# Query and key projections by Strassen's scheme in a stage of their own, behind the values

## The chip, the cores and the metric

The kernel runs on one core of a Trainium2 chip. The engines are TensorE (PE: matmuls, with PEld for its weight loads), VectorE (DVE), ScalarE (ACT), GpSimd (POOL) and SyncE (SP, which here only issues DMAs). The time is that of one execution on the device, in microseconds; lower is better.

## The reference

One layer of a decoder trunk, 1024 tokens by 1024 channels, float32. Only the first half of the layer matters here. One projection of the normalised input gives everything that the mixer needs:

```python
h = rms_norm(x, pre_mix_g[l])
proj = h @ w_in[l]                         # (1024, 1024) @ (1024, 8192)
qa, ka, va, qb, kb, vb, gates = jnp.split(proj, split_at, axis=-1)
qa = apply_rope(qa.reshape(b, s, A_HEADS, 2, A_QK_DIM), cos_a, sin_a)     # 4 heads, 2 x 64
ka = apply_rope(ka.reshape(b, s, A_HEADS, 2, A_QK_DIM), cos_a, sin_a)
...
oa = diff_attention(qa, ka, va, lam)       # causal (softmax1 - lam * softmax2) @ v
...
qb = apply_rope(qb.reshape(b, s, B_GROUPS, B_HEADS, B_HEAD_DIM), cos_b, sin_b)   # 3 groups, 4 heads of 128
kb = apply_rope(kb.reshape(b, s, B_GROUPS, B_HEADS, B_HEAD_DIM), cos_b, sin_b)
...                                        # windows (128, 512, 2048) with dilation (1, 4, 16)
mix = (g_a * ya + g_b * yb) @ w_mix_out[l] # g_a, g_b: sigmoid of the gates
x = x + rms_norm(mix, post_mix_g[l])
...                                        # then a gated MLP with a short convolution
```

So queries and keys are 2 x 512 columns for attention A and 2 x 1536 for attention B: 32 blocks of 128 columns. The gates are 16 more blocks.

## The kernel before

Every float32 product is made of three matmuls with operands split in two parts: high (a rounded copy, made by ScalarE) and low (the rest, a subtraction by VectorE). `split` makes both parts, `mm3` (lines 153 to 157) issues the three matmuls high x high, low x high and high x low.

The program is written in order, and a scheduler turns it into one fixed stream of instructions for each engine, by a simulated time line and by priorities (`high_priority`), and by explicit ties (`issue_after`: an instruction may be placed only after another one). At run time each engine works through its stream in order and waits on semaphores. A tile pool hands out a fixed number of buffers for each tag; a write into a buffer waits until the last reader of its earlier content is done.

The stages up to the mixer's output are these.

- The values (lines 445 to 654). The 2048 value columns are computed by Strassen's scheme: seven products of half-sized blocks in place of eight. The input x stands transposed in SBUF, split in `xh` and `xl`, channels in two halves and tokens in two halves: blocks b11, b12, b21, b22. The scheme needs sums of these blocks. They are t2, t3, t4 in tiles of their own, and t1, which takes the place of b12. At the end of this stage b12 is loaded and split again (`again`), because all that follows needs the plain x. The norms of the rows, the rotation tables (`tab_d`) and the softmax weight lambda are made beside it. The values go to HBM (`v_d`).
- Queries, keys and gates (`proj_t`, lines 232 to 244). A block of 128 columns is computed in two halves of 512 tokens, each a sum over eight channel blocks: 2 x 8 x 3 = 48 matmuls of 128x512, with weights in `load_unit`, loaded by SP and split. A yield after every six matmuls lets a caller interleave it with other work.
- Attention A (`attend_a`, from line 749): four heads, each with eight blocks of 128 query rows in the order 6, 7, 4, 5, 2, 3, 0, 1. A job is one such block: scores into two PSUM buffers, mask and minimum (VectorE), two exponentials (ScalarE), the weighted difference (VectorE). Its transposes, splits and products with the values follow one to two jobs later (`later`).
- Attention B (`attend_b`, from line 950): twelve steps (two pairs of heads, three groups, two heads), each with four jobs of two row blocks, and a merge of the three groups' results by their log-sums.
- The output projections, the mixer and the MLP. The MLP's up projection uses Strassen's scheme too (`seven`, from line 1437), with 84 matmuls to a step.

The order around the change is this. While attention A works on head h, `interleave` puts the projections of head h+1 (`proj_a`) and three gates between the jobs, in proportion to weights; in attention B it puts the projections of the next step (`proj_b`). Queries and keys go from PSUM through `rotated` (a copy of swapped halves by ScalarE; two products with the tables and a sum by VectorE) and are split straight into the SBUF tiles that the scores read. These tiles, the values of a pair of heads and the raw values come from one pool of 18 buffers (`slot`). Gates are stored to HBM (`gt_d`) and read again by the output projections. The distribution of the gates is written by hand:

```python
START_GATES, A_FILLS, B_GATES = 1, ("gpgg", "gpvgg", "wgpgg", "xgPVgg"), 3
```

Here p and P stand for projections, g for a gate, v and x for loads of values, w and V for splits of them.

## Time and profile before

| | |
|---|---|
| median of 3 runs | 1696.86 us (1695.76 to 1697.7) |
| the profiled execution | 1697.3 us, span 1695.3 us |
| TensorE busy | 1682.1 us, 99% of the span, 8078 matmuls |
| VectorE busy | 1333.5 us, 79%, 2445 instructions |
| ScalarE busy | 891.8 us, 53%, 1663 instructions |
| GpSimd busy | 106.3 us, 6%, 174 instructions |
| HBM traffic | 167.05 MB read, 47.86 MB written |
| TensorE's mean granted clock | 0.998 |

A line of the profile names the engine and the line of the kernel, the tile written and the tiles read ("acc<-xh,whi": the accumulator from x's high part and a weight's high part), the shape, and how often it ran. A line can be that of a helper: L155 to L157 are the three matmuls of `mm3`, wherever it was called; L149 and L146 are the copy and the subtraction of `split`. "<-" behind an idle time names what ended it. Busy time is the union of an engine's instructions; matmuls of 128x512 overlap, so a sum of their durations is more than the time that they take. In a table of stretches the columns are the stretch, its length, the busy time and number of instructions of each engine, the granted clock, the share of the DMA engines' time and GB/s.

### The profile page before, as it was taken

The page shows a single profiled execution, that of the slowest core. Times are in us where ns is not written, and L with a number is a line of the kernel's source. Part 1 is how long each engine was busy: PE and PEld are TensorE (multiplying, and loading weights), DVE is VectorE, ACT ScalarE, POOL GpSimd, SP SyncE. Part 2 cuts the span into 40 slices and gives each one's busy share as a digit, 9 for nine tenths or more (in the row PEclk, how much of TensorE's full clock was granted, in tenths as well). Part 3 has the DMA queues.
Part 4 walks back from the last instruction along what each step waited for, and adds up shares of the span by engine and source line. Part 5 has one row for each costly group of instructions (what it writes and reads, how often), then busy time and mean ns, then how long its engine had stood idle before and what let it go on. Part 6 is the DMA issues. An engine that isn't in the chain of part 4 may idle for free.

```text
span 1695.3 us, 22960 instructions
## 1 busy us (share of the span) xinstructions
PE 1682.1 (99%) x8078; PEld 1410.0 (83%) x8078; DVE 1333.5 (79%) x2445; ACT 891.8 (53%) x1663; POOL 106.3 (6%) x174
## 2 busy tenths in 40 slices
PE   9999999999999999999999999999999999999997
PEld 7888888888888888888888888888888888888886
DVE  8795686877776766677756865899999989799967
ACT  7643575656454776666653533464444445355453
POOL 0031000000000000000123400300000000000000
PEclk9999999999999999999999999999999999999999
DMA  8677311214112213233585631132222222296524
GB/s 266 234 253 235 99 60 62 86 59 119 50 63 81 70 53 108 86 112 119 200 285 186 203 118 63 38 106 92 95 81 75 98 83 88 95 343 214 193 75 161
DMA packets 104451, 216.41 MB, mean 128 GB/s; under 512 B 12992, under 2 KB 22144, under 8 KB 104336
## 3 DMA queue, kind: packets, MB, share of 16 engines
q1 hardware_dynamic: 89296, 171.28, 30.5%
q0 software_dynamic: 10288, 35.28, 6.1%
q10 hardware_dynamic: 4752, 8.39, 1.3%
q8 instruction: 63, 1.03, 0.3%
q14 instruction: 52, 0.43, 0.1%
HBM read 167.05 MB, written 47.86 MB: 127 GB/s over the span
## 4 chain that ended last, share of the span: by engine, by line
PE 97%; DMA 2%; DVE 1%; ACT 1%; issue 0%; SPq 0%; DVEq 0%
PE acc L155 22%; PE acc L156 22%; PE acc L157 22%; PE acc L1578 3%; PE acc L1579 3%; PE acc L1577 3%; PE o L710 2%; PE pt L697 2%; PE acc L1258 2%; PE acc L1256 2%; PE acc L1257 2%; PE o L713 1%; PE s L156 1%; PE s L157 1%; PE s L155 1%; PE s L768 1%
## 5 line engine op out<-in xcount | busy, mean ns | idle before, releaser
L156 PE MATMUL acc<-xh,wlo 128*128 128x512 f32 x768 | 303.2, 395 | 0.0
L157 PE MATMUL acc<-xl,whi 128*128 128x512 f32 x768 | 303.1, 395 | 0.0
L155 PE MATMUL acc<-xh,whi 128*128 128x512 f32 x768 | 303.0, 395 | 0.0
L149 ACT ACTIVATE whi<-raw 128x512 fp32r<-128x512 f32 (+1 forms) x252 | 156.1, 626 | 170.3 <-PE acc L157 88.1
L146 DVE TENSOR_TENSOR wlo<-raw,whi 128x512 fp32r<-128x512 f32 (+1 forms) x252 | 178.8, 717 | 40.4 <-ACT whi L149 34.7
L156 PEld LDWEIGHTS acc<-xh,wlo 128*128 128x128 f32 x768 | 144.4, 188 | 27.8
L157 PEld LDWEIGHTS acc<-xl,whi 128*128 128x128 f32 x768 | 144.5, 188 | 27.5
L155 PEld LDWEIGHTS acc<-xh,whi 128*128 128x128 f32 x768 | 144.4, 188 | 27.3
L155 PE MATMUL acc<-mh,whi 128*128 128x512 f32 x400 | 155.8, 390 | 0.3 <-ACT mh L149 0.3
L156 PE MATMUL acc<-mh,wlo 128*128 128x512 f32 x400 | 155.6, 389 | 0.0
L157 PE MATMUL acc<-ml,whi 128*128 128x512 f32 x400 | 155.3, 389 | 0.0
L684 ACT ACTIVATE t<-acc 64x512 f32<-64x512 f32 (+1 forms) x160 | 94.7, 592 | 55.3 <-PE acc L157 53.3
L1454 DVE TENSOR_TENSOR u<-acc,u 128x512 f32<-128x512 f32 x133 | 91.3, 691 | 20.3 <-PE acc L157 20.1
L149 ACT ACTIVATE whi<-s 128x512 fp32r<-128x512 f32 x76 | 46.9, 627 | 102.3 <-PE acc L157 88.1
L685 DVE TENSOR_TENSOR t<-acc,cos 128x512 f32<-128x512 f32 x64 | 44.1, 690 | 67.1 <-ACT t L684 63.5
L155 PEld LDWEIGHTS acc<-mh,whi 128*128 128x128 f32 x400 | 75.1, 188 | 16.0 <-ACT mh L149 0.5
L156 PEld LDWEIGHTS acc<-mh,wlo 128*128 128x128 f32 x400 | 75.1, 188 | 15.6
L157 PEld LDWEIGHTS acc<-ml,whi 128*128 128x128 f32 x400 | 75.1, 188 | 15.5
L1578 PE MATMUL acc<-whi,wlo 128*128 128x512 f32 x220 | 77.6, 390 | 0.0
L1577 PE MATMUL acc<-whi 128*128 128x512 f32 x220 | 76.4, 389 | 0.0
L1579 PE MATMUL acc<-wlo,whi 128*128 128x512 f32 x220 | 73.2, 390 | 0.0
L777 ACT ACTIVATE s<-s,mx 128x896 f32<-128x896 f32 (+7 forms) x64 | 49.4, 772 | 36.9 <-DVE mx L770 21.0
(387 smaller groups left out, 3941.6 us busy)
## 6 DMA issues: line engine op xcount, KB each, us to landing
raw<-in_w_in SPq DMA_DIRECT2D x96, 256.0 KB, 2.9
raw<-in_w_up SPq DMA_DIRECT2D x88, 256.0 KB, 2.8
raw<-in_w_v SPq DMA_DIRECT2D x71, 256.0 KB, 4.7
raw<-c_d SPq DMA_DIRECT2D x48, 256.0 KB, 3.8
c_d<-c SPq DMA_DIRECT2D x22, 512.0 KB, 2.7
raw<-in_w_down SPq DMA_DIRECT2D x37, 256.0 KB, 4.1
v_d<-yv POOLq DMA_DIRECT2D x32, 256.0 KB, 4.5
gt_d<-gate ACTq DMA_DIRECT2D x32, 256.0 KB, 2.1
```

Of the source, the lines that this page charges most:

```text
L146: eng.tensor_tensor(lo, src, hi.bitcast(F32), op=ALU.subtract)
L149: copy = nc.scalar.activation(hi, src, AF.Copy)
L155: nc.tensor.matmul(o, sh, mh, start=first, stop=False, skip_group_check=on)
L156: nc.tensor.matmul(o, sl, mh, start=False, stop=False, skip_group_check=on)
L157: nc.tensor.matmul(o, sh, ml, start=False, stop=last, skip_group_check=on)
L684: nc.scalar.activation(t1[dst], ps[src], AF.Copy)
L685: nc.vector.tensor_tensor(t2, ps, cos[:, sl], op=ALU.mult)
L777: exp = nc.scalar.activation(sc[c][:, :w], sc[c][:, :w], AF.Exp, bias=mx[:, c, 0:1], scale=-1.0, accum_out=den[:, c : c + 1])
L1454: nc.vector.tensor_tensor(to, made(p), x, op=ALU.add)
L1577: nc.tensor.matmul(banks[m], gh[:, tk], wh, start=f == 0, stop=False)
L1578: nc.tensor.matmul(banks[m], gl[:, tk], wh, start=False, stop=False)
L1579: nc.tensor.matmul(banks[m], gh[:, tk], wl, start=False, stop=f == NH - 1)
```

## The change

The projections of queries and keys leave the attention stages and become one stage between the values and attention A.

- The stage works on 16 pairs, a query block and its key block: four heads of A, then twelve of B in the order of their use. A pair's 256 columns by 1024 tokens are computed by Strassen's scheme (`seven_q`): seven products of 4 x 3 matmuls with the blocks of x that the values used, t1 still in the place of b12. Two products add to a bank of another (p2 on p1, p3 on p5). So the loading and splitting of b12 moves from the end of the values to the end of this stage.
- The sums of weight blocks are made by DMA. SP loads a11, a12, a22 and a21; ScalarE writes negated copies; DMAs that accumulate, issued by GpSimd, add blocks: s1 = a21 + a22, s3 = a11 - a21, s2 = s1 - a11, s4 = a12 - s2 (`sums_a` two pairs ahead, `sums_b` one). Pair 0's are begun in the last steps of the values, and its weights split there. Seven weight tiles of a pair are split while the pair before is computed (`put_w`).
- A pair's results are rotated in SBUF (`rotate_q`, tiles of 128x1024) and split and stored to HBM (`store_q`, into the new `qk_d`) while the next pair is computed. For this the rows of w_in's query and key blocks are permuted on the host for heads of A, and unpermuted by the store.
- `in_turn` ties the stage's ScalarE and VectorE instructions to each other in the written order; only the evictions stand outside of it, with a higher priority.
- The attention stages load queries and keys from `qk_d` (`load_a`: twelve DMAs of 64 rows; `load_b`: four of 512 KB), one head or step ahead.
- The gates are the only projections left between the jobs. They are handed out in pieces of six matmuls: 8 before attention A, 16 in each of its heads, 4 or 5 in each step of B. A piece is tied behind the first score matmuls of the job before the last (`scored`, `issue_after`).
- The products with the values alternate between two pools of PSUM (`outs`). The rotation tables lie in a pool that is open from the start.

```diff
-START_GATES, A_FILLS, B_GATES = 1, ("gpgg", "gpvgg", "wgpgg", "xgPVgg"), 3
+START_GATES, B_GATES = 8, (4, 5, 4, 5, 5, 5, 4, 5, 5, 5, 4, 5)
+A_FILLS = ("gpggg", "gpgvgg", "wgpggg", "xgPgVgg")
...
+    qk_d = dram.tile([2 * (AH + BG * BH), 2, P, S], F32, name="qk_d")
...
+    outs = itertools.cycle([lambda: psum(F32, ps_o, "o"), psum])
...
+    def in_turn():
+        with ExitStack() as stack:
+            for ins in tail.values():
+                stack.enter_context(tc.issue_after(ins))
+            last = nc.cur_bb.bb.instructions[-1]
+            yield
...
+                if ins.engine in (nc.scalar.engine, nc.vector.engine):
+                    tail[str(ins.engine)] = ins
...
+        def sums_a(n):
+            d11, d12, d21, d22 = quarters(n)
+            to = sums_q[n] = {"a11": load_raw(d11, "raw"), "s1": begin(d21), "a22": load_raw(d22, "t1"), "a12": load_raw(d12, "t2")}
+            to["s3"] = begin(to["s1"], -1.0)
+            to["s2"] = begin(to["a11"], -1.0)
+            add_to(to["s1"], d22)
+            add_to(to["s3"], d11)
+            add_to(to["s2"], to["s1"])
...
+        def put_w(n, *names):
+            for name in names if n < len(pairs) else ():
+                t = ws_q.setdefault(n, {})[name] = next(slots_q)()
+                split(*t, sums_q[n][name])
...
-            if (p, i) == ("p5", 1):
-                again.append(load_raw(a["xT"][k][:, 512:], next(tags)))
-            if (p, i) == ("p6", 1):
-                with behind_marks():
-                    split_x(k, halves()[1], again[k])
...
+        ops_q = dict(p1=("a11", b11), p6=("s2", t2), p2=("a12", b21), p7=("s3", t3), p5=("s1", b12), p4=("a22", t4), p3=("s4", b22))
...
+        def rotate_q(n, c, u):
+            sw = pq.tile([P, S], F32, tag="sw", name="sw", bufs=2)
+            for src, dst in ((up_half, low_half), (low_half, up_half)):
+                nc.scalar.activation(sw[dst], u[src], AF.Copy)
+            nc.vector.tensor_tensor(u, u, tab[0], op=ALU.mult)
+            nc.vector.tensor_tensor(sw, sw, tab[1], op=ALU.mult)
+            nc.vector.tensor_tensor(u, u, sw, op=ALU.add)
...
+            m1 = made("p1")
+            copy(c11, m1)
+            yield
+            m4 = made("p4")
+            made("p2", m1)
+            m6 = made("p6")
+            add(c12, m6, c11)
+            copy(c11, m1)
+            yield
+            m7 = made("p7")
+            add(c22, m7, c12)
+            add(c21, m4, c22)
+            yield
+            m5 = made("p5")
+            add(c22, m5, c22)
+            yield us
+            made("p3", m5)
+            add(c12, m5, c12)
+            yield
...
+            next(made_q)
+            if n:
+                next(before)
+                with in_turn():
+                    rotate_q(n - 1, 1, old[1])
+            with in_turn():
...
+                put_w(n + 1, "a11")
+                for m, fn in ((n + 1, sums_b), (n + 2, sums_a)) if n else ((2, sums_a),):
+                    if m < len(pairs):
+                        fn(m)
+            if n:
+                with in_turn():
+                    store_q(n - 1, 1, old[1])
...
+            if n == len(pairs) - 1:
+                again = [load_raw(a["xT"][k][:, 512:], t) for k, t in enumerate(("raw", "t1", "t2", "raw"))]
+                with in_turn():
+                    for k in range(4):
+                        split_x(k, halves()[1], again[k])
...
+    def load_a(h, res):
...
+            dma(f32(to), src)
...
+                with tc.issue_after(scores[0]) if scores[0] else nullcontext():
+                    piece = next(supply, None)
...
+    def load_b(g, h, res):
+        ops = [slot(n) for n in ("qh", "ql", "kh", "kl")]
...
+            dma(f32(t), qk_d[at + n // 2, n % 2])
...
-        fill = proj_b(nxt[1], nxt[2], ops_b[nxt], functools.partial(split_b, *nxt[:2]) if h % 2 else None)
-        interleave(jobs(todo), 4, (itertools.chain(fill, once(load_ots)) if nxt == steps[-1] else fill, 8))
+        fills = [(once(functools.partial(load_b, *nxt[1:], ops_b[nxt])), 0), gates(B_GATES[n] // 2)]
+        if h % 2:
+            fills.append((once(functools.partial(split_b, *nxt[:2])), 0))
+        fills.append(gates(B_GATES[n] - B_GATES[n] // 2))
```

248 lines of the change are left out of this document (168 added, 80 removed).

## The prediction

> **What bounds the kernel now.** I read the page's engine totals and its chain first, then the table of stretches over the stages that the change touches, then the rows of single tiles in those stretches.
>
> ```profile
> PE 1682.1 (99%) x8078; PEld 1410.0 (83%) x8078; DVE 1333.5 (79%) x2445; ACT 891.8 (53%) x1663; POOL 106.3 (6%) x174
> ...
> PE 97%; DMA 2%; DVE 1%; ACT 1%; issue 0%; SPq 0%; DVEq 0%
> ```
>
> TensorE is busy for 99% of the span and is 97% of the chain that ended last. So a matmul that goes away is worth its time, as long as nothing else becomes late. The stretches are the values (to 162 us), the first gate and head 0's projections (to 204), differential attention (to 504) and dilated attention (to 864); columns are length, busy time by engine, clock, DMA share, GB/s.
>
> ```profile
> 0.00:162.00 162.00, 158.92 (x689) 130.46 (x690) 130.63 (x229) 89.87 (x154) 23.77 (x46) 1.00 0.74 245
> 162.00:204.00 42.00, 42.00 (x187) 34.80 (x186) 20.00 (x31) 22.15 (x37) 2.47 (x6) 1.00 0.42 133
> 204.00:504.00 300.00, 300.00 (x1570) 256.15 (x1569) 228.62 (x585) 174.20 (x364) 0.00 (x0) 1.00 0.23 73
> 504.00:864.00 360.00, 360.00 (x1985) 309.49 (x1984) 248.59 (x566) 233.33 (x500) 22.20 (x38) 1.00 0.34 112
> ```
>
> From 162 to 864 us, 702 us, TensorE has no idle time at all at full clock. VectorE (DVE) has 76% and 69% of the two attention stretches.
>
> The same table restricted to the accumulators "acc" counts the projection's matmuls in the attention stretches (PE is the second number):
>
> ```profile
> 204.00:504.00 300.00, 235.88 (x944) 172.62 (x943) 27.53 (x40) 33.07 (x56) 1.00 0.23 73
> 504.00:864.00 360.00, 293.74 (x1174) 213.35 (x1173) 33.71 (x49) 52.20 (x88) 1.00 0.34 112
> ```
>
> Busy times of pipelined matmuls overlap, so the price is the distance of their starts:
>
> ```profile
> 265.69 0.39 PE L156 MATMUL acc<-xh,wlo 128*128 128x512 f32 x1
> ...
> 269.33 0.39 PE L157 MATMUL acc<-xl,whi 128*128 128x512 f32 x1
> ```
>
> These are the first and last of 17 in a row: 3.64 us over 16 steps, 0.2275 us each. Differential attention then holds 944 x 0.2275 = 214.8 us of projections and 85.2 us of its own; dilated attention 267.1 and 92.9 us. This is the filler: 6.7 us for each of 32 jobs (4 heads x 8 row blocks), 5.6 us for each of 48 (12 steps x 4).
>
> **The change part by part.** *Matmuls removed.* Queries and keys are 32 column blocks of 2 x 8 x 3 = 48 matmuls, 1536. A pair (query and key block) becomes seven products of 4 x 3 matmuls, 84 in place of 96, so 16 x 84 = 1344. 192 go, all of 128x512: 192 x 0.2275 = 43.7 us. The gates stay 16 x 48. New TensorE time for this part: 305.8 (new stage) + 174.7 (gates) + 178.1 (attention) = 658.6, against 702. A gain beyond 43.7 us is excluded, since TensorE had no idle time in these stretches to win back.
>
> *The new stage: who keeps up.* A pair has 84 x 0.2275 = 19.1 us of TensorE. DVE's prices come from back-to-back starts:
>
> ```profile
> 1314.46 0.69 DVE L1454 TENSOR_TENSOR u<-acc,u 128x512 f32<-128x512 f32 x1
> 1315.06 0.68 DVE L146 TENSOR_TENSOR wlo<-raw,whi 128x512 fp32r<-128x512 f32 x1
> ```
> ```profile
> 609.01 2.36 DVE L146 TENSOR_TENSOR vl<-vperm,vh 128x1024 fp32r<-128x1024 f32 x2
> 611.29 0.55 DVE L146 TENSOR_TENSOR pt<-pt 128x384 fp32r<-128x384 f32 x1
> ```
> ```profile
> 602.05 1.21 DVE L878 TENSOR_TENSOR ql<-t,qh 128x512 fp32r<-128x512 f32 x1
> 603.15 0.70 DVE L146 TENSOR_TENSOR wlo<-raw,whi 128x512 fp32r<-128x512 f32 x1
> ```
>
> So 0.60 us for 512 columns, 1.14 for 1024, 1.10 for 512 read with a stride. A pair has 7 weight splits and 5 evicting adds (12 x 0.60 = 7.2), 6 rotation operations and 2 store splits of 1024 columns (8 x 1.14 = 9.1): 16.3 us, 85% of 19.1. For the eight pairs with dilation 4 or 8 the store splits are strided, 2.2 us each: 7.2 + 6.8 + 4.4 = 18.4 us, 96%. Is that enough? The kernel has such a stage, the same 84 matmuls to a step, in its up projection:
>
> ```profile
> 1110.00:1180.00 70.00, 70.00 (x310) 57.76 (x309) 69.97 (x100) 34.98 (x54) 0.81 (x9) 1.00 0.30 106
> 1180.00:1250.00 70.00, 70.00 (x311) 57.98 (x309) 66.07 (x90) 30.06 (x40) 0.80 (x8) 1.00 0.26 87
> ```
>
> There TensorE loses nothing beside a DVE that is 100% and 94% busy. If DVE lost its overlap (durations 0.69, 1.18, 2.3 in place of starts), a strided pair would need 8.3 + 7.1 + 4.6 = 20.0 us, 0.9 too much, 7 us over eight pairs. I take 3, nearer to the up projection's row; ends 0 and 7. ScalarE:
>
> ```profile
> L149 ACT ACTIVATE whi<-raw 128x512 fp32r<-128x512 f32 x40 | 25.1, 629 | 15.2 <-PE acc L157 14.7
> ...
> L149 ACT ACTIVATE vh<-vperm 128x1024 fp32r<-128x1024 f32 x6 | 6.3, 1051 | 0.1
> ```
>
> 12 operations of 512 columns (7 splits, 2 evictions, 3 negated sums) and 6 of 1024 (4 half-swaps, 2 store copies): 7.5 + 6.3 = 13.8 us, some 2 us more with strides, 72 to 83%. It hides. The sums ride on DMAs. Accumulating ones aren't in this trace; the nearest rows:
>
> ```profile
> raw<-in_w_in SPq DMA_DIRECT2D x96, 256.0 KB, 2.9
> ...
> v_d<-yv POOLq DMA_DIRECT2D x32, 256.0 KB, 4.5
> ...
> ot<-oa_d SPq DMA_DIRECT2D x4, 512.0 KB, 4.0
> ```
>
> s1 is a load and one accumulate, s2 one more: 2.9 + 4.5 + 4.5 = 11.9 us (2.9 + 2 x 2.9 = 8.7 at the lower end), and ScalarE needs s2, to begin s4, one iteration (19.1 us) after the issue. So I cost them at nothing, hidden by one pair of TensorE. POOL issues four per pair; in the values they stand behind the stores to v_d, with one whole pair before s2 is due. Stage traffic is 4 MB in 19.1 us, 210 GB/s, against 245 in the values: it fits.
>
> *Start and end of the stage.* Pair 0's first sums and seven splits (7 x 0.60 = 4.2 us of DVE) lie at the end of the values, where DVE is 81% busy; the re-split of x leaves there. I take 1 us, ends 0 and 4.2. At the other end TensorE has only the last product (2.7 us) and 8 gate pieces (8 x 6 x 0.2275 = 10.9), 13.6 us in all, while DVE still owes the last pair's rotations and stores (6.8 + 4.4), four splits of x (2.4) and two of values (2.3): 15.9 us before the first masks. SP must also bring 1 MB of values and head 0's twelve 256 KB parts, 4 MB, 16 us at 245 GB/s, into slots that come free after product p7, 16.4 us before the gates run out. Both are just about as long as the cover. I take 6 us; ends 0, and 14 if the first scores come after the whole cover.
>
> *Attention without projections.* What leaves it are operations on the rotated tile "t" (first two rows: DVE, then ACT) and splits of "raw" weights (last two):
>
> ```profile
> 204.00:504.00 300.00, 60.56 (x91) 58.30 (x97) 0.00 (x0) 1.00 0.23 73
> 504.00:864.00 360.00, 130.83 (x176) 96.94 (x132) 0.00 (x0) 1.00 0.34 112
> ```
> ```profile
> 204.00:504.00 300.00, 27.48 (x40) 25.14 (x40) 1.00 0.23 73
> 504.00:864.00 360.00, 33.27 (x48) 30.50 (x48) 1.00 0.34 112
> ```
>
> Differential attention keeps 85.2 us and gets 64 gate pieces of 6 matmuls (87.4): 172.6 us of TensorE, 5.4 per job. DVE keeps 228.6 - 60.6 - 27.5 = 140.5, 8 gate evictions go and 16 splits come (+5): 146, 85%. ScalarE: 174.2 - 58.3 - 25.1 + 16 x 0.63 = 101, 58%. Dilated attention: 92.9 + 56 pieces (76.4) = 169.3 us, 3.5 per job; DVE 248.6 - 130.8 - 33.3 + 19 = 103, 61%; ScalarE 233.3 - 96.9 - 30.5 + 12 = 118, 70%. No engine is over its time; what can be late is one job's chain. In A, the last score of a 1024-wide job to the end of its combination:
>
> ```profile
> 226.91 0.39 PE L768 MATMUL s<-l,q 128*128 128x512 f32 x1
> ```
> ```profile
> 234.54 1.28 DVE L784 SCALAR_TENSOR_TENSOR s<-s,ratio 128x1024 f32<-128x1024 f32 x1
> ```
>
> 8.9 us (with rotations queued in between that will be gone). Four score tiles hold two jobs, 10.8 us, so it is covered; with no overlap the end is 32 x (8.9 - 5.4) = 112. I take 6, near the covered end, for uneven jobs. In B, last score, end of the exponentials, split of the turned block:
>
> ```profile
> 565.32 0.28 PE L157 MATMUL s<-kl,qh 128*128 128x256 f32 x1
> ```
> ```profile
> 566.70 0.19 ACT L981 ACTIVATION_READ_ACCUMULATOR bs<-bs,stat 128x1 f32 x1
> ```
> ```profile
> 569.01 0.55 DVE L146 TENSOR_TENSOR pt<-pt 128x384 fp32r<-128x384 f32 x1
> ```
>
> 4.2 us, spread over two further jobs (7 us): covered; at one job of overlap the end is 48 x 0.7 = 34. I take 5. Reloads are 3 MB in a head's 43 us and 2 MB in a step's 14; at 4.0 us per 512 KB one after another, four take 16 us, overlapped less: inside the 5. The last step shrinks from 3 gates of filler (32.8 us) to 5 pieces (6.8), with four splits of oa and a merge in it: 2 us, ends 0 and 8.
>
> *Sum.* Against the profiled execution's own 1697.3 (span 1695.3; the runs' median is 0.4 less): 1697.3 - 43.7 + 3 + 1 + 6 + 6 + 5 + 2 = 1676.6, 1676 on the median's scale. All lower ends give 1653.6.
>
> A rule that speaks against the change: the Trainium skill, "Perfetto Trace Analysis", Optimization Strategy, says that a kernel whose busiest engine differs by stage may gain by interleaving the stages. Here the interleaving of projections and attention is undone. By that rule the first rival below would come about; this trace only shows the interleaved state, without idle time.
>
> **The rivals.** *Attention runs dry (slower).* Filler per job falls from 6.7 to 2.7 us in A and from 5.6 to 1.6 in B. If a job's chain is exposed, TensorE idles before the transposes. The other terms cost 12, so slower begins at (43.7 - 12) / 80 = 0.40 us per job. At 0.7 us: 1697.3 - 43.7 + 12 + 56 = 1722. For it: ScalarE at 70% and DVE at 85% in strict order. Against: the two-job covers above. *All of it arrives.* If attention loses nothing and the rest 4: 1658. For it: the up projection's rows. *Late sums.* If an accumulate takes over (19.1 - 3.5) / 2 = 7.8 us, ScalarE waits for s2 in its fixed order with the evictions behind it; at 10 us, 4.4 us for each of 15 pairs, 66: 1743. Against: 4.5 us in the row. *The clock drops.* Only the last stretch shows it, at 0.82 where TensorE has little to do:
>
> ```profile
> 1680.00:1695.00 15.00, 5.48 (x25) 4.20 (x23) 10.55 (x28) 2.06 (x7) 0.00 (x0) 0.82 0.73 250
> ```
>
> If 16 stage, head and step boundaries each cost 18% of 15 us, 43 us: 1720. It needs waits of some us, which I don't expect. The Trainium skill, "TensorE: Matmul & The Clock Gate", HAM oscillation, gives half the clock after an idle window of about 3.4 us; by it my estimate would be 1.7 us each, 27 in all, 1704.
>
> **How the numbers follow.** Forecast 0.48 (its own range 1665 to 1690), all of it arrives 0.20, attention dry 0.22, late sums 0.06, clock 0.04. 0.2% is 3.4 us, about what a measurement can tell here. Faster: 0.48 + 0.20 + 0.04 of a mild dry case; same 0.05 at its edge; slower the rest, 0.23. The range 1655 to 1716 leaves out the dry case's upper part, late sums and the very best end, under 0.2.
>
> **What would show it.** TensorE matmuls fall by 192. Right: the new stage takes 306 to 313 us with TensorE at 9 in every slice and DVE at 9; some idle us where attention begins; A 173 to 185, B 169 to 180. Wrong: matmuls of attention or transposes named as waiting for ScalarE or DVE for over 35 us in total; a ScalarE wait on an accumulating DMA; a clock under 1.

## The result and the profile after

The changed kernel takes 1789.95 us (median of 4 executions, 1787.54 to 1792.65) against 1696.46 us for the kernel before: a ratio of 1.0551, 95% interval 1.0532 to 1.0569. The forecast was 1676 us with a range of 1655 to 1716; the kernel became 5.5% slower. (Of the runs below, one execution of e13_fill_start and one of e15_three_fill were slow, 5825 and 3943 us; they are left out of all numbers.)

The first row is from the page of the kernel after, engine totals: busy time, share of the span, instructions; the second is its chain of work that ended last, by engine.

```profile
PE 1682.5 (94%) x7886; PEld 1393.6 (78%) x7886; DVE 1384.6 (77%) x2413; ACT 906.3 (51%) x1633; POOL 163.6 (9%) x238
...
PE 72%; DMA 9%; DVE 7%; ACT 5%; issue 5%; SPq 1%; DVEq 0%; POOL 0%; ACTq 0%; POOLq 0%
```

The 192 matmuls are gone (8078 to 7886), and TensorE's busy time is still what it was, 1682.1 before and 1682.5 now. So the saving of 43.7 us was eaten by matmuls that ran longer, and the idle time of TensorE, span minus busy, rose from 13.2 to 105.2 us: 92.0 us, which is the loss. Where it lies shows in the table of stretches of the kernel after (columns as in the prediction: length, busy time by engine, granted clock, DMA share, GB/s). The stretches are the new stage, the first gate pieces, differential attention (A), dilated attention (B), the output projections, and the rest.

```profile
162.00:498.00 336.00, 314.57 (x1344) 253.08 (x1342) 268.05 (x308) 212.92 (x281) 55.56 (x65) 0.98 0.71 190
498.00:536.00 38.00, 15.13 (x55) 11.64 (x56) 23.17 (x26) 15.76 (x17) 0.58 (x1) 0.72 0.71 222
536.00:747.00 211.00, 189.39 (x1003) 157.75 (x1003) 148.70 (x461) 98.28 (x240) 0.54 (x1) 0.94 0.45 127
747.00:932.00 185.00, 175.44 (x1128) 156.56 (x1128) 99.78 (x337) 108.39 (x319) 13.20 (x22) 0.96 0.74 257
932.00:1137.00 205.00, 189.59 (x847) 155.86 (x846) 137.68 (x236) 86.90 (x161) 45.16 (x54) 0.97 0.52 183
1137.00:1788.00 651.00, 639.77 (x2825) 528.18 (x2823) 580.35 (x825) 295.54 (x466) 20.42 (x45) 0.99 0.35 120
```

Read each row against what TensorE needs there by the prediction's own working (180 us for the output, its length before):

| stretch | needs | takes | idle | busy beyond its need |
|---|---|---|---|---|
| new stage | 305.8 | 336 | 21.4 | 8.8 |
| first gate pieces | 10.9 | 38 | 22.9 | 4.2 |
| A | 172.6 | 211 | 21.6 | 16.8 |
| B | 169.3 | 185 | 9.6 | 6.1 |
| output | 180 | 205 | 15.4 | 9.6 |
| sum | 838.6 | 975 | 90.9 | 45.5 |

The sum is 136.4 us over the need: the 92.4 us by which the span grew, the 43.7 us that were to be won, and 0.3 us of rounding. No single stretch carries it. Note that no other engine is full in any of these rows: VectorE (the third number) has 268 of 336 us in the new stage, 149 of 211 in A.

The longest wait stands at the start of A. The lines are TensorE's in order of time: start, duration, instruction, and in brackets the idle time before it and what ended it.

```profile
517.29 0.39 PE L157 MATMUL acc<-xh,wlo 128*128 128x512 f32 x1
517.52 0.39 PE L158 MATMUL acc<-xl,whi 128*128 128x512 f32 x1
535.68 1.08 PE L939 MATMUL s<-k,q 128*128 128x512 f32 x2 [17.77 <-DMA k<-qk_d]
536.56 0.63 PE L156 MATMUL acc<-xh,whi 128*128 128x512 f32 x1
536.99 0.63 PE L157 MATMUL acc<-xh,wlo 128*128 128x512 f32 x1
...
545.78 1.08 PE L942 MATMUL s<-l,q 128*128 128x512 f32 x2 [1.86 <-DMA l<-qk_d]
```

Two things are to be seen. The load of k, which stood under the cover of the gate pieces in the prediction, is 17.8 us late. And the matmuls behind the wait start 0.43 us apart, not 0.23 as before it: half the clock. The Trainium skill, "TensorE: Matmul & The Clock Gate", HAM oscillation, gives half the clock behind an idle window of some 3.4 us. The trace agrees in kind; a sharp bound it does not show, see the last section.

### The profile page after: what moved, and what is told of

Read it like the earlier page. It is cut to its first block, busy times and chain, and to the rows that moved or that the text cites. A ratio compares the mean times of both kernels' runs of the same rounds, so it can differ in the third digit from the quotient of the medians.

```text
span 1787.7 us, 23232 instructions
## 1 busy us (share of the span) xinstructions
PE 1682.5 (94%) x7886; PEld 1393.6 (78%) x7886; DVE 1384.6 (77%) x2413; ACT 906.3 (51%) x1633; POOL 163.6 (9%) x238
## 4 chain that ended last, share of the span: by engine, by line
PE 72%; DMA 9%; DVE 7%; ACT 5%; issue 5%; SPq 1%; DVEq 0%; POOL 0%; ACTq 0%; POOLq 0%
PE acc L156 13%; PE acc L157 13%; PE acc L158 13%; PE acc L1759 2%; PE acc L1760 2%; PE acc L1761 2%; PE s L156 2%; PE s L157 2%; PE s L158 2%; PE acc L1438 2%; PE acc L1440 2%; PE acc L1439 2%; PE pt L157 2%; PE pt L156 2%; PE pt L158 2%
## 5 line engine op out<-in xcount | busy, mean ns | idle before, releaser
L150 ACT ACTIVATE whi<-s 128x512 fp32r<-128x512 f32 x140 | 82.4, 623 | 143.0 <-PE acc L158 103.0
L156 PE MATMUL acc<-xh,whi 128*128 128x512 f32 x352 | 143.3, 408 | 6.2 <-ACT whi L150 4.9
L157 PE MATMUL acc<-xh,wlo 128*128 128x512 f32 x352 | 143.3, 407 | 4.1 <-DVE wlo L147 4.1
L158 PE MATMUL acc<-xl,whi 128*128 128x512 f32 x352 | 141.6, 403 | 0.0
L1636 DVE TENSOR_TENSOR u<-acc,u 128x512 f32<-128x512 f32 x133 | 91.3, 691 | 21.2 <-PE acc L158 21.0
L147 DVE TENSOR_TENSOR wlo<-s,whi 128x512 fp32r<-128x512 f32 x140 | 93.1, 687 | 8.8 <-ACT whi L150 8.3
L156 PEld LDWEIGHTS acc<-mh,whi 128*128 128x128 f32 x400 | 75.1, 188 | 15.9 <-ACT mh L150 0.5
L156 PEld LDWEIGHTS acc<-xh,whi 128*128 128x128 f32 x352 | 69.2, 197 | 20.8 <-ACT whi L150 5.6
L157 PEld LDWEIGHTS acc<-xh,wlo 128*128 128x128 f32 x352 | 69.1, 196 | 19.3 <-DVE wlo L147 6.0
L944 DVE CUSTOM_DVE_ANT_0 s<-s,mask_a 128x512 f32<-128x512 f32 (+3 forms) x96 | 51.8, 554 | 37.2 <-PE s L942 25.6
L158 PEld LDWEIGHTS acc<-xl,whi 128*128 128x128 f32 x352 | 68.8, 195 | 14.0
L150 ACT ACTIVATE qkh<-u 128x1024 fp32r<-128x1024 f32 x32 | 50.5, 1577 | 51.3 <-DVE u L743 42.9
```

What stands on the lines that cost most here:

```text
L147: eng.tensor_tensor(lo, src, hi.bitcast(F32), op=ALU.subtract)
L150: copy = nc.scalar.activation(hi, src, AF.Copy)
L156: nc.tensor.matmul(o, sh, mh, start=first, stop=False, skip_group_check=on)
L157: nc.tensor.matmul(o, sl, mh, start=False, stop=False, skip_group_check=on)
L158: return nc.tensor.matmul(o, sh, ml, start=False, stop=last, skip_group_check=on).ins
L944: nc.vector.tensor_tensor_reduce(out=s_sb[:, c0:c1], in0=ps, in1=mask, scale=-scale, scalar=3.0e38, op0=ALU.add, op1=ALU.min, accum_out=mx ...
```

## The experiments

Each experiment changes the kernel after. The table gives the median, the ratio to the kernel before with its interval, and from one profile the time of A's first score, then the lengths from there to B's first score, to the first output projection, and to the first up projection. Kernels whose edits lie elsewhere show how far these lengths scatter from one profile to the next: A's 212 to 219, B's 179 to 185, the output's 205 to 207. Less than that is no finding. The rest, 648 to 652 us in all of them, isn't touched.

| run | time | ratio | A starts | A | B | output |
|---|---|---|---|---|---|---|
| after | 1790.0 | 1.0551 (1.0532-1.0569) | 535.7 | 211.8 | 184.7 | 204.8 |
| e1_free | 1786.6 | 1.0535 (1.0507-1.0562) | 531.7 | 213.1 | 183.4 | 206.1 |
| e2_nostride | 1769.8 | 1.0434 (1.0417-1.0450) | 520.9 | 214.0 | 180.6 | 205.7 |
| e3_pool | 1788.3 | 1.0540 (1.0524-1.0557) | 534.4 | 218.1 | 179.3 | 205.3 |
| e4_nosums | 1780.1 | 1.0488 (1.0470-1.0506) | 524.7 | 214.4 | 183.0 | 205.9 |
| e5_first | 1777.9 | 1.0476 (1.0457-1.0495) | 523.4 | 214.4 | 179.9 | 205.7 |
| e6_more_in_a | 1811.3 | 1.0672 (1.0656-1.0688) | 535.4 | 267.7 | 158.3 | 197.9 |
| e7_few_loads | 1775.3 | 1.0461 (1.0446-1.0477) | 533.0 | 210.1 | 178.0 | 201.4 |
| e8_last | 1776.6 | 1.0478 (1.0458-1.0498) | 535.7 | 214.0 | 187.3 | 187.1 |
| e9_stage | 1752.4 | 1.0327 (1.0311-1.0342) | 495.8 | 218.8 | 179.3 | 207.2 |
| e10_no_combination | 1771.0 | 1.0430 (1.0414-1.0445) | 537.9 | 192.5 | 180.5 | 205.6 |
| e11_two | 1769.3 | 1.0422 (1.0404-1.0439) | 526.0 | 216.5 | 188.3 | 186.4 |
| e12_three | 1776.2 | 1.0466 (1.0450-1.0483) | 531.5 | 218.0 | 191.2 | 187.0 |
| e13_fill_start | 1792.3 | 1.0558 (1.0544-1.0571) | | | | |
| e14_fill_a | 1793.2 | 1.0562 (1.0548-1.0575) | 538.7 | 221.6 | 183.9 | 197.0 |
| e15_three_fill | 1776.3 | 1.0463 (1.0436-1.0490) | 523.7 | 227.2 | 191.4 | 182.7 |
| e16_fill_look | 1786.9 (one) | | 535.0 | 215.2 | 180.6 | 204.7 |
| e17_all_out | 1706.9 | 1.0065 (1.0048-1.0082) | 497.1 | 189.1 | 183.0 | 185.5 |

### The new stage: the written order, the strides, the sums (e1, e2, e4)

Who waits in the stage shows in the waits of all engines between 162 and 498 us of the kernel after: engine, line and tile, what it waited for, us in total, times, longest.

```profile
ACT qkh L150 <- DVE u L743: 42.1, 20, 3.8
...
ACT s L647 <- DMA s<-in_w_in: 17.8, 8, 4.3
DVE qkl L147 <- ACT qkh L150: 16.9, 18, 2.7
```

ScalarE's copy of a rotated block waits for VectorE's rotation, VectorE's difference for that copy. TensorE's own waits in the same stretch all end on VectorE, 21.2 of its 21.4 us of idle time: on weight splits (9.5 us, first row) and on adds that free an accumulator (11.7 us, second row).

```profile
PE acc L157 <- DVE wlo L147: 6.0, 6, 1.3
PE o L156 <- DVE u L762: 4.6, 1, 4.6
```

Is it the order that ties the engines, the length of the work, or the sums? A's first score also moves with what happens behind the stage, so the stage's own length is needed too. It runs from the start of its first product to the start of the first gate piece, less the wait before that piece. In the kernel after:

```profile
161.77 0.39 PE L156 MATMUL pt<-xh,whi 128*128 128x512 f32 x1
...
502.83 1.22 PE L156 MATMUL acc<-xh,whi 128*128 128x512 f32 x2 [4.91 <-ACT whi L150]
```

| run | the stage ends | its length | over its need of 305.8 |
|---|---|---|---|
| after | 497.9 | 336.1 | 30.3 |
| e2_nostride | 486.5 | 325.0 | 19.2 |
| e4_nosums | 488.8 | 327.3 | 21.5 |
| e9_stage (below) | 471.5 | 310.1 | 4.3 |
| e11_two (below) | 501.0 | 338.2 | 32.4 |
| e12_three (below) | 488.9 | 327.5 | 21.7 |

e1 drops the ties between the pieces:

```diff
-            for ins in tail.values():
-                stack.enter_context(tc.issue_after(ins))
```

> The ties between ScalarE's and VectorE's instructions in the new stage are taken away; the scheduler places them by its own simulated time. Theory A, the written order costs the stage: ScalarE waited 42 us for rotated tiles and VectorE 17 us for high parts while TensorE waited for both, so the stage (336 us from its first matmul to its last, 306 of them needed) shrinks by 15 us or more and the kernel comes to about 1770. Theory B, VectorE has too much to do in the dilated pairs: nothing changes by more than 5 us. Theory C, the order is what keeps the stage together: it grows by over 10 us.

The time stays within 4 us. These ties are not the cause. (Each engine still has a fixed order, now the scheduler's own.)

e2 reads the rotated blocks without a stride in the store split:

```diff
-            if dil == 1:
+            if True:
                 split(hi, lo, u)
```

> The dilated pairs' results are split and stored in plain order, so their store splits read without a stride (the reordering by residues is left out, so attention B works on other data). Theory B, load: sixteen ScalarE copies of 2.1 us and sixteen VectorE subtractions of 2.1 us fall to about 1.1 us; if the dilated pairs are what VectorE can't keep up with, the stage loses 16 us or more of its 30 us excess and the kernel comes to about 1770. Theory A, written order alone: under 6 us, since pairs without a stride waste as much.

20 us come back in the median and 16 between the profiled executions. A's first score is 14.8 us earlier, and the stage is 11.1 us shorter; the rest is spread over stretches within their scatter. The strided operations are this cost: in the kernel after the copy of 1024 columns takes 2.0 to 2.2 us on ScalarE and the difference as long on VectorE, 1.06 and 1.22 without a stride.

e4 takes the accumulating loads out:

```diff
-            nc.gpsimd.dma_start(t, src, accum_op=ALU.add)
+            pass
```

> The accumulating DMAs are left out (the weight sums are then only their first terms, so queries and keys are wrong numbers of the same kind). Theory F, late sums: ScalarE's waits for the sums in its fixed order (17.8 us for loaded sums, 2.2 us for accumulated ones) hold back evictions and splits; the stage shrinks by 10 us or more, to about 1775. Theory A or B: under 5 us.

10 us come back, A's first score is 11.0 us earlier, and the stage is 8.8 us shorter. The sums that the prediction costed at nothing cost about this much. That they come late is not shown to be the reason. The 17.8 us that ScalarE waits in the view above are for SyncE's plain loads of a21; 14.1 us of them stay in e4. For accumulated sums ScalarE waits 2.2 us in the kernel after. The edit takes 64 transfers and their traffic away as well, and what it is in them that costs stays open.

### The start of A: a queue, or memory (e3, e5)

e3 issues the loads of the first values and of head 0 from GpSimd's queue, in the same order:

```diff
-        of_first = fetch_values(1, 0)
+        of_first = fetch_values(1, 0, nc.gpsimd.dma_start)
...
-        load_a(0, ops[0])
+        load_a(0, ops[0], nc.gpsimd.dma_start)
```

> Only the first two loads of values and the twelve loads of head 0's queries and keys are issued by GpSimd in place of SyncE. TensorE waited 17.8 us for them; in SyncE's stream they stand behind the last pair's stores and were issued from 521 us on. Theory D, queue order: they are issued about 20 us earlier, the 17.8 us wait falls under 5 and with it some matmuls at half clock; the kernel comes to 1765 to 1773. Theory E, memory: the buffers come free only when the last pair is stored; the loads are issued at 515 us or later and the time stays within 4 us.

Nothing moves, and the rows of these loads say why (instructions of that line in the kernel of e3, and what ended the idle time before them):

```profile
L864 POOL DMA_DIRECT2D vperm<-v_d x2: 786/792/797, 515.4 to 520.1; - x2
its engine sat idle before it (us, times) until:
  DVE u L743: 26.1, 1
```

GpSimd stood before the values' load for 26 us; it waited for VectorE's last rotation, so the tile takes memory that the last pair still uses. Are head 0's six tiles free earlier, so that their twelve loads only stand behind this one? e5 turns the two around:

```diff
...
-        of_first = fetch_values(1, 0)
+        of_first = [slot("vperm", (P, 4, 256), F32) for _ in range(2)]
         vs[0] += [v_tiles() for _ in range(2)]
-        load_a(0, ops[0])
+        load_a(0, ops[0], nc.gpsimd.dma_start)
+        fetch_values(1, 0, nc.gpsimd.dma_start, of_first)
```

> Edit: the twelve loads of head 0's queries and keys, and then the first two loads of the values, go through GpSimd's queue instead of SyncE's; in the changed kernel the values' loads stood first. The first values' tile lies over a rotation buffer and a split buffer of the last pair, so its load can't start before that pair is rotated and stored; the twelve tiles of head 0 lie over the sums of x, which the last product leaves at about 498. Theory memory-and-queue: the 17.8 us that TensorE waits for k of head 0 are there only because those loads stand in a queue behind something that waits for the last pair; now they are issued from 490 to 505 and the wait falls to 5 us or less. First score at 518 to 523 instead of 535.7, time 1770 to 1778. Theory data (the rival): the loads are late for another cause (the transfers themselves, in the crowd of the last stores), and the wait stays over 12 us, time 1784 to 1790.

The wait for k falls to 5.2 us, A starts 12.3 us earlier, and the time falls by as much, close to what was expected. But it is not for the expected reason. Head 0's loads were to go out from 490 to 505 us, because the last products free their tiles. They too waited for VectorE's last rotation. The first and the last of them, in GpSimd's order of time, in e5 and then in e3:

```profile
515.64 1.08 POOL L919 DMA_DIRECT2D q<-qk_d  x2 [25.84 <-DVE u L743]
...
523.57 0.51 POOL L919 DMA_DIRECT2D l<-qk_d  x1 [1.51 <-DMA k<-qk_d]
```
```profile
520.86 1.09 POOL L919 DMA_DIRECT2D q<-qk_d  x2
...
534.64 0.53 POOL L919 DMA_DIRECT2D l<-qk_d  x1 [0.96 <-DMA k<-qk_d]
```

So the order in the queue is what e5 wins: without the values' loads ahead of them, the first goes out 5 us earlier and the last 11 us. That the memory is held until the last rotation stays.

### Attention: filler, loads, chain (e6, e7, e10)

e6 moves 48 gate pieces from B into A:

```diff
-START_GATES, B_GATES = 8, (4, 5, 4, 5, 5, 5, 4, 5, 5, 5, 4, 5)
+START_GATES, B_GATES = 8, (0, 0, 0, 0, 0, 0, 0, 0, 0, 0, 0, 8)
...
-                "g": lambda: gates(4),
+                "g": lambda: gates(7),
```

> Edit: all gate pieces but 16 are worked off in the attention of the first kind (7 instead of 4 for each place in it), 8 ahead of it as before, 8 in the very last step of the second kind; the other eleven steps of that kind get none. Theory lead: an attention step is idle because its chain (scores, maxima, exponentials, combination, transposes) is longer than the PE work that now stands between two steps; with 48 pieces (66 us) more in it, the first kind's excess over its PE work falls from 39 us to under 20 (its length is 172.6 + 65.5 + under 20 = under 258), and the second kind's, which now has nearly no filler, grows from 15 to over 40. Theory traffic (the rival): the excess comes from the reloads and stays at 30 to 40 us in the first kind (268 to 278 long), and the second kind's stays at 10 to 20. The time tells little by itself; by lead it is 1785 to 1830.

The stretches of A and of B in that kernel:

```profile
535.00:803.00 268.00, 249.76 (x1296) 209.15 (x1297) 169.41 (x498) 107.54 (x253) 0.54 (x1) 0.96 0.45 137
803.00:961.00 158.00, 133.75 (x844) 122.42 (x842) 87.51 (x313) 104.39 (x315) 14.79 (x25) 0.83 0.71 253
```

A is 29.6 us over its need (172.6 + 65.5 = 238.1), between what the two theories gave; B, left with almost no filler, is 54.5 us over its own (169.3 - 65.5 = 103.8), as the theory of the lead said. So B lives by its filler. A gains some 10 us by filler and keeps the rest.

e7 leaves the reloads out:

```diff
-            dma(f32(to), src)
+            if h == 0:
+                dma(f32(to), src)
+        for to in res if h else ():
+            nc.gpsimd.memset(f32(to), 0.01)
...
-            dma(f32(t), qk_d[at + n // 2, n % 2])
+            nc.gpsimd.memset(f32(t), 0.01)
```

> Edit: the queries and keys of heads 1 to 3 of the first kind and of all twelve of the second aren't loaded again: GpSimd fills their tiles with a constant instead (so the scores are not the reference's); about 36 MB of reading goes, from 521 to 915. Theory traffic: what the attention lost over its PE work (39 us in the first kind, 15 in the second) is the price of these reloads, and at least 25 of the 54 us come back: time 1755 to 1765. Theory lead: the steps are idle for their own chains, and the attention gains 0 to 12 us: time 1776 to 1790.

The time falls by 14.7 us, just below what the lead gave. A is 1.7 us shorter although the DMA share there falls from 0.45 to 0.23; the rest is 2 to 7 us in each of the other stretches, hardly more than their scatter. For A the theory of traffic falls. Where the 14.7 us lie is not settled.

What TensorE waits for in A, in the kernel after, is, beside the loads, one thing: the transposes of a head's widest pair of blocks, and later of a narrow one. The waits' row, and the longest of them in order of time:

```profile
PE pt L884 <- DVE s L958: 14.7, 7, 4.3
```
```profile
562.32 1.54 PE L884 MATMUL pt<-ident,s 128*128 128x128 f32 x6 [4.35 <-DVE s L958]
```

L958 is the combination of the two halves. e10 leaves it out:

```diff
-        nc.vector.scalar_tensor_tensor(sc[0][:, :w], sc[1][:, :w], ratio, sc[0][:, :w], op0=ALU.mult, op1=ALU.add)
```

> Edit: in the attention of the first kind the combination of the two halves' weights (32 VectorE instructions of 0.4 to 1.3 us) is left out, and the transposes take the first half's exponentials as they are (another result). Theory chain: the first kind's 39 us over its PE work come from the step's chain (scores, maxima, two exponentials, combination, transposes), which is longer than the 12 fill matmuls behind the scores; 1.3 us less of it in each of 16 pairs and VectorE less loaded take most of the waits of the transposes (14.7 us) with the half clock behind them: the stretch from the first score of the first kind to the first of the second falls from 211.8 to under 198, time 1770 to 1778. Rival, placement: the fill stands in the wrong places whatever the chain costs, the transposes now wait for the exponentials instead, and the stretch stays over 203, time 1780 to 1788.

A takes 192.5 us, 19.3 less, and the time 19.0 less. TensorE's waits in A after that edit:

```profile
PE s L939 <- DMA k<-qk_d: 19.5, 2, 16.9
PE s L939 <- DVE mx L944: 3.7, 9, 0.9
PE s L942 <- DMA l<-qk_d: 2.4, 1, 2.4
PE pt L884 <- ACT s L951: 2.0, 1, 2.0
```

The transposes waited 14.7 us for the combination (7 times); now they wait 2.0 us, once, for the exponentials. About half of A's 39 us over its need goes with this one operation. The edit shortens a job's chain and unloads VectorE at once; the two aren't told apart.

### The last step (e8)

e8 moves seven gate pieces from the earlier steps of B into its last one:

```diff
-START_GATES, B_GATES = 8, (4, 5, 4, 5, 5, 5, 4, 5, 5, 5, 4, 5)
+START_GATES, B_GATES = 8, (4, 4, 4, 4, 4, 4, 4, 4, 4, 4, 4, 12)
```

> Edit: the second kind's steps get 4 gate pieces each and the last of them 12 (in the changed kernel 4 or 5 each, 5 in the last). Theory short-last-step: the output stage lost 24.5 us because the last step, which was 24 matmul groups long before, is now so short that the third head's merge and the gates' loads behind it on GpSimd's queue fall into the output projection; with 7 pieces (9.6 us) more in it the stretch from the first output projection to the first up-projection loses 8 us or more of its 204.8, the attention of the second kind gets at most 3 us longer than by its PE work, and the time is 1778 to 1786. Rival (the gates' loads or the merge are late for their own length, whatever stands before): the stretch stays over 200 and the time is 1787 to 1795.

The output takes 187.1 us instead of 204.8. The first row is the kernel after, the second e8, both from TensorE's waits in the output projections: an accumulator that the gated product frees late. (The gates' loads stand behind the last merge's in GpSimd's queue.)

```profile
PE acc L156 <- DVE ya L1374: 7.9, 1, 7.9
```
```profile
PE acc L156 <- DVE ya L1374: 2.0, 1, 2.0
```

The wait shown explains 5.9 of the 17.7 us. TensorE's idle time in the stretch falls from 15.4 to 4.1 us, its busy time from 189.6 to 182.9. B is 2.6 us longer, and the seven pieces moved gave 13.4 us of the time.

### Do they add up? (e9, e11, e12)

e9 is e2, e4 and e5 in one.

> Edit: three earlier edits together: the split of the turned pairs reads without a stride (these groups' columns then lie in another order), the sums of weights take only their first term (no accumulating DMA), and head 0's loads go ahead of the values' through GpSimd's queue. Theory separate causes: the first alone brought the first score forward by 14.8 us, the second by 11.0, the third by 12.3; if each has a cause of its own, it now comes 38 us earlier, at 498, and the time is 1748 to 1756. Theory one slack: the load of ACT and VectorE and the late sums are the same wait seen twice, and the first score comes at 503 to 511, the time 1757 to 1768.

A starts at 495.8, 39.9 us earlier; the three alone gave 14.8 + 11.0 + 12.3 = 38.1. They are separate causes. The time falls by 37.6 us, and the stage is left 4.3 us over its need. e5 by itself leaves the stage's length as it is (336.1), so the strided operations and the accumulating loads together are 26 of the 30 us.

e11 joins e5 and e8, the two that leave the kernel's output as it is.

> Edit: the two that gave time back and change no result, together: head 0's queries and keys loaded first, through GpSimd's queue, and twelve gate pieces in the last step of the second kind, four in each of the others. They act 400 us apart, so they should add: 1790.0 - 12.1 - 13.4 = 1764, 1760 to 1769. If less than 18 us come back, one of them was paid for by something that the other moves.

20.7 us come back of 25.5, just beyond the upper end of the expected times.

e12 adds to e11 a turned copy on ScalarE, so that VectorE reads without a stride:

```diff
-                split(*(t.rearrange("p (r i) -> p r i", r=dil) for t in (hi, lo)), u.rearrange("p (i r) -> p r i", r=dil))
+                nc.scalar.activation(f32(lo).rearrange("p (r i) -> p r i", r=dil), u.rearrange("p (i r) -> p r i", r=dil), AF.Copy)
+                split(hi, lo, f32(lo))
```

> Edit: as the run with two, and for the pairs with a stride ACT first writes the rotated pair in its turned order into the low part's tile, and the split then reads and writes that without a stride (one strided ACT copy of some 2.1 us and a plain one of 1.06 in place of a strided one; VectorE's difference 1.22 instead of 2.14). Theory load of VectorE: VectorE, at 81% in the stage, is what the order waits for; 32 strided differences less save 29 us of it, 32 plain copies more cost ACT (at 64%) 34, and the time falls by 5 to 12 us below the run with two. Theory load of both: what counts is the path through ACT and VectorE together, which gets no shorter (0.1 us longer for each tile), and the time is within 3 us of the run with two, or longer.

(The text's 32 tiles are 16: eight pairs of two.) The time is 6.9 us longer than e11's, and A starts 5.5 us later. Read by the time alone, relieving VectorE doesn't help. The stage says otherwise: it takes 327.5 us where e11's takes 338.2, although ScalarE has more to do in it (224 us busy for 214) and the path of a block through both engines is no shorter. So VectorE's strided differences alone held the stage up by some 10 us, and the theory of VectorE's load was right about the stage. What it won is lost behind the stage. The first row is from e11, the others from e12:

```profile
526.01 1.08 PE L939 MATMUL s<-k,q 128*128 128x512 f32 x2 [4.52 <-DMA k<-qk_d]
```
```profile
518.38 0.55 POOL L1352 DMA_DIRECT2D gl<-gt_d  x1 [61.61 <-DVE qkl L147]
...
531.54 1.09 PE L940 MATMUL s<-k,q 128*128 128x512 f32 x2 [17.62 <-DMA k<-qk_d]
```

In e12's stream for GpSimd a load of gates stands ahead of head 0's loads, and it waits for VectorE's very last difference. Head 0's loads go out from 519.4 to 531.7 us (518.1 to 526.2 in e11), and the wait for k is 17.6 us again.

### The clock (e13 to e16)

Does the clock fall because TensorE stood idle, and what does it cost? e13 fills the 17.8 us hole with matmuls that nobody reads:

```diff
...
+        with tc.issue_after(mms[-1]):
+            idle = psum(F32, pt, "pt")
+            for _ in range(70):
+                warm.append(nc.tensor.matmul(idle, xh[:, 0, :P], xh[:, 0, :512], start=True, stop=True).ins)
```

> Edit: 70 matmuls that nobody reads (128x512, 0.2275 us each at full clock, 15.9 us) stand between the first gate pieces and the first score, where TensorE waits 17.8 us for k of head 0 in the changed kernel; nothing else moves. Theory idle-then-half-clock: the granted clock falls because TensorE stood idle, so with the hole filled the first scores run at full clock: granted clock of the 20 us from the first score over 0.9 instead of 0.69, and the useless 15.9 us cost nothing or pay 2 to 4 us: time 1785.5 to 1789.5. Rival, clock by load or by chance: the useless matmuls change nothing on the clock of the stretch behind them (0.65 to 0.75), time 1789 to 1793.

Four executions take 1790.2 to 1793.9 us: no gain. e16 is the same kernel, for its profile.

> Edit: the kernel of the run with the filled start once more, for its profile: 70 matmuls that nobody reads where TensorE waits 17.8 us for k of head 0. Theory idle-then-half-clock: granted clock of the 20 us from the first score over 0.9 instead of 0.69, and TensorE's busy time over the whole span rises by less than the 15.9 us put in (1682.5 + 15.9 - 2 to 4 = 1694 to 1696). Rival, clock by chance: clock 0.65 to 0.75 there, busy time 1697 to 1700.

The 20 us from the first score on, first in the kernel after, then in e16:

```profile
535.70:555.70 20.00, 16.55 (x44) 11.71 (x45) 7.50 (x23) 3.54 (x6) 0.00 (x0) 0.68 1.04 242
```
```profile
535.00:555.00 20.00, 14.29 (x50) 10.21 (x51) 7.52 (x23) 3.54 (x6) 0.00 (x0) 0.91 1.04 244
```

The granted clock is 0.91 in place of 0.68, and TensorE gets more matmuls done in less busy time. Over the whole span its busy time is 1692.2 us, 9.7 more for 15.9 put in. So the low clock followed from the idle time. And it costs nothing here. In e16 the next parts of k and l set the pace:

```profile
538.76 0.64 PE L944 MATMUL s<-l,q 128*128 128x512 f32 x2 [1.72 <-DMA l<-qk_d]
...
545.66 0.47 PE L944 MATMUL s<-l,q 128*128 128x512 f32 x1 [2.28 <-DMA l<-qk_d]
```

The second stands at 545.66; in the kernel after it stood at 545.78, at half clock up to there. The stretched matmuls filled a wait that was there anyway.

e14 puts such matmuls behind the scores whose transposes wait, eight in each of two places per head:

```diff
+        if i in (3, 7):
+            with tc.issue_after(back.ins):
+                idle = psum(F32, pt, "pt")
+                for _ in range(8):
+                    nc.tensor.matmul(idle, xh[:, 0, :P], xh[:, 0, :512], start=True, stop=True)
```

> Edit: in the attention of the first kind 8 such matmuls (1.8 us) stand behind the scores of the two steps in each head whose transposes wait for the combination (0 and 1.2 to 4.35 us each in the changed kernel): 64 in all, 14.6 us of useless work. Theory idle-then-half-clock: they lie in the waits (14.7 us in all) and keep the clock up behind them, so the stretch from the first score of the first kind to the first of the second gets shorter in spite of them, 200 to 209 instead of 211.8, time 1779 to 1788. Rival, waits alone: the waits fall by what is put in and the clock's part is no matter; the stretch is 211 to 217, time 1789 to 1796.

A takes 221.6 us, 9.8 more for 14.6 us of useless work, more than either theory gave, and the time is 3.2 us longer. The clock in A stays at 0.94. (The output is 7.8 us shorter in this kernel, with a wait for "ya" of 2.7 us in place of 7.9. Why is not known.) e15 adds it to e11.

> Edit: the run with two (head 0's loads first, twelve gate pieces in the last step) and the useless matmuls of the attention's run. If the clock theory holds they add to 1757 to 1767, below the 1769.3 of the run with two; if it doesn't, 1769 to 1777. No theory brings it under the 1697 of the kernel before.

1776.3 us (1766.6 to 1782.2) against 1769.3: not below. So useless work in A does not pay. The share of the clock in the loss remains unsettled: that it follows the idle time is shown, that curing it alone wins time was not found in either place.

### Everything at once (e17)

The edits of e2, e4, e5, e7, e8 and e10 together.

> Edit: everything at once that an earlier run took out or mended: no stride in the splits, no accumulating sums, head 0's loads first through GpSimd's queue, no combination in the attention of the first kind, no reloads of queries and keys but head 0's, twelve gate pieces in the last step (another result). Theory separate places: the stage and the transition gave 37.6 us, the last step 13.4, the combination 19.0, the reloads 14.5, of which some 4 lay in the transition that is gone already; 1790.0 - 80 = 1710, 1702 to 1720, and TensorE's busy time falls from 1682.5 towards the 1638.4 that it would be at full clock, to under 1660. Theory one slack (each edit shortens the same waits): 1725 to 1745.

1706.9 us, where the sum of the parts gave 1710. Its engine totals:

```profile
PE 1656.9 (97%) x7886; PEld 1381.9 (81%) x7886; DVE 1340.3 (79%) x2381; ACT 887.3 (52%) x1631; POOL 174.7 (10%) x254
```

The named causes account for 83 of the 93 us lost, and even without all of them, and without a good deal of the work, this version stands 0.65% above the kernel before. The other 54 us between it and the 1653 that all lower ends of the prediction's terms give are 18 us of TensorE beyond 1638.4 (1682.1 - 43.7) and some 35 us of idle time (1705.0 - 1656.9 = 48.1, 13.2 of them as before).

## Why the prediction was wrong

**Right.** The 192 matmuls went, and the two ends did not change: 162 us of values, 651 us from the first up projection. VectorE and ScalarE stay below their time in every stretch, as computed. Of the signs that the prediction named as wrong, the clock under 1 came plainly (0.974). Of the other two little came: TensorE waited 28.4 us in the two attentions for VectorE and ScalarE, not over 35, and ScalarE waited 2.2 us for accumulating DMAs.

**The step that failed** is the price of the cover: five terms, 3 + 1 + 6 + 6 + 5 + 2 = 23 us, measured at 136. In the forecast's order:

- *The stage, 3 + 1 (ends 0 to 11.2), measured 30* (161.8 to 497.9 against 305.8). The argument was the up projection, where TensorE loses nothing beside a VectorE that is 100% busy. It doesn't carry over. In the new stage VectorE is 80% busy, and still 21.2 of TensorE's 21.4 idle us end on it. e9 shows what makes it so: without the strided operations and the accumulating loads 4.3 of the 30 us are left. The strides alone give 11.1 (e2), and 10.7 by VectorE's part of them (e12 against e11). e1 shows that it isn't the ties. Why VectorE is late with a fifth of its time free is not settled; it waits itself 16.9 us for ScalarE's copies of the rotated blocks.
- *Sums at nothing, measured about 10, within the 30 above.* The bound that was set, 7.8 us per accumulate, wasn't reached: they land in 5.3. So the rival "late sums" didn't come about, and the sums weren't free either; e4 shows the price and not its reason.
- *The transition, 6 (ends 0 to 14), measured 27* (497.9 to 535.7 less 10.9 of gate pieces). "Slots that come free after product p7" was false: the values' loads (e3) and head 0's (e5) both wait for VectorE's last rotation, to 515 us, when the cover is all but over. And the values' loads stand ahead in the queue; that order is 12 us of it (e5). 5 us are a wait for the gates' weights.
- *A, 6 (ends 0 to 112), measured 39; B, 5 (ends 0 to 34), measured 15.* The cover was reckoned in mean jobs (5.4 us for each of 32). But a head's jobs are 1024 to 128 columns wide, and the chain of the widest stands behind 12 matmuls of filler, 2.7 us. The rival "attention runs dry" gave 56 us for this, and 54 came. Its mechanism is borne out by the transposes' waits and by e10, which takes 19 of A's 39 us away. Its size is in part luck: it priced 0.7 us for every job, and A lost 1.2 per job, B 0.3. The reloads, which were counted inside B's 5, are 14.7 us by e7, in places that it doesn't settle. The prediction gave the rival 0.22 and let the two-job covers speak against it; the missing look was at the narrowest place rather than at the mean.
- *The end, 2 (ends 0 to 8), measured 24.5.* It was reckoned inside the last step. The work pushed out of it fell into the output projection, a stretch that the prediction didn't cost at all. e8 gives 17.7 of it back.
- *The clock, at nothing with 0.04.* TensorE's busy time shows 44 us of stretched matmuls, near the prediction's 43 us for that rival. The closeness is luck: that sum went by 18% of 15 us at 16 boundaries, which no run shows. And they partly lie in waits (e16), so they don't add to the terms above: the terms above include them.

The rule set against the change, the Trainium skill, "Perfetto Trace Analysis", Optimization Strategy, that interleaving stages with different busy engines may gain, agrees with the result: undoing an interleaving in which TensorE had no idle time cost 92 us of idle time.

## What to carry to other kernels

When work that fills gaps is taken out of a chain-bound stage, price the stage by its tightest place (widest job, the filler that really stands behind it) and not by mean busy shares: TensorE waited for a VectorE that was 80% busy. Follow a piece that shrinks to the next stage as well, and look up in the trace what a transfer waits for before it is called early. Judge an edit by its own stage and not only by the time: what e12 won in its stage was lost right behind it. An edit that removes 2.6% of the bound engine's work needs the other engines on time, and not only below full.

## What the runs showed of the hardware

- Half the clock behind waits: behind 17.77 us the starts are 0.43 us apart instead of 0.23. It also came behind a wait of 1.97 us and not behind one of 1.96 us (six transposes in 1.54 and 0.88 us):

```profile
576.64 0.88 PE L884 MATMUL pt<-ident,s 128*128 128x128 f32 x6 [1.96 <-DVE s L958]
...
682.11 1.54 PE L884 MATMUL pt<-ident,s 128*128 128x128 f32 x6 [1.97 <-DVE s L958]
```

Behind another wait of 1.97 us, at 628.31, the six took 0.87 us. So the idle time just before it alone doesn't decide. With the hole filled the clock stayed up (0.91 against 0.68).
- Reading 1024 columns with a stride of 4 or 8 elements takes ScalarE's copy from 1.06 to between 2.0 and 2.2 us, and VectorE's difference from 1.22 to as much.
- An accumulating load of 256 KB of the weights landed in 5.3 us (median of 48), a plain load of that size into the same kind of tile in 6.4 (median of 16, issued by SyncE).
